# The first 24 microseconds of a hybrid attention and recurrence block: second token block in halves, weight split on three engines, projection steps between transposes

## The chip, the cores and the metric

The kernel runs on one core of a Trainium2 chip. The metric is the device time of one execution in microseconds (us). The core's engines are TensorE (PE: matrix products and transposes, with the weight loads shown apart as PEld), VectorE (DVE), ScalarE (ACT), GpSimd (POOL) and SyncE (SP, which here only issues DMAs). Each engine runs its own instructions in order; semaphores make it wait for the others.

## The reference

One layer on 1024 tokens of width 1024, all in float32:

```python
xn = rmsnorm(x, norm1_g[layer])
u = xn @ w_in[layer].astype(f32)
q_sb, k_sb, v_sb, f_raw, i_hg, q_hg, g_hg, gate_sb, gate_hg = jnp.split(u, list(c), axis=-1)
o_sb = stick_breaking_attention(...)        # 8 heads of 64, needs q_sb, k_sb, v_sb
o_hg = hgrn2_chunkwise(...)                 # 4 heads of 128
merged = g_a * (o_sb @ w_o_sb) + g_b * (o_hg @ w_o_hg)
h = x + merged @ w_out
h = h + square(relu(rmsnorm(h, norm2_g) @ w_ff1)) @ w_ff2
return rmsnorm(h, final_g)
```

The change touches only the beginning: the root-mean-square norm of the tokens, its transposition, and the first projections (query and key of head 0, and v of all heads).

## The kernel before, in words

**Split operands.** Products are made in fp32r, a rounded form of float32. To keep the accuracy each operand is split into a high part (a cast to fp32r, made by ACT, `hi_copy`, L155) and a low part (the source minus the high part, made by DVE, `lo_sub`, L158), and each product is three matmuls, high x high, high x low and low x high (`three`, L566). So ACT and DVE have to feed PE with two tiles per operand.

**Token blocks.** The tokens lie in 8 blocks `x0` to `x7` of 128 rows (tokens) by 1024 columns. A block is normed by its own rows: the sum of squares of each row, then the power -0.5 of it on POOL (`inv_root`, L272), giving one factor per row (`n_y` in the profile), then a scaling of the block in place. For blocks 0 to 3 ACT squares the left half of a block and DVE the right half (`half_means`, L621); an addition on DVE joins the two sums. PE transposes the scaled blocks in 128x128 pieces into PSUM (`xnt`, `norm_transpose`, L322); out of PSUM ACT makes the high part times the norm's gain (`xnh`, L348) and DVE the low part (`xnl`, L351). There are 8 column blocks, called kt; one PSUM bank takes a column block of all token blocks that are transposed together (two in the front). The kernel's pool of PSUM banks has 8.

**The first job.** `first_job` (L724) makes the projections that come first, in steps that the main program orders with `st.advance(n, ...)`: (1) query and key of head 0 for blocks 0 and 1, four steps of two kt each (`pjqk` in the profile, 24 products of 128x256); (2) a part of v for blocks 0 and 1, kt 0 to 3, in four quarters: both products with the high weights for kt 0 and 1, the same for kt 2 and 3, then the product with the low weights for kt 0 and 1, and for kt 2 and 3 (`pjv`, 128x512); (3) query and key for blocks 2 and 3, four steps; (4) the rest, beginning with the epilogue of query and key (two casts on ACT, two subtractions on DVE, and two DMAs from POOL's queue that copy rows 0 to 63 to rows 64 to 127, L682).

The weights of query and key, `wqk0r`, come in four DMAs, two for each half (kt 0 to 3, kt 4 to 7), and are split in two halves (`FirstUnit.split`, L717): high parts `wqk0whi` on ACT, low parts `wqk0wlo` on DVE. The weights of v, `wvr`, come in four pieces of two kt each and are split into `wvh` and `wvl`; the low part of the second piece is put off (`owed_wlo`, L487) until `lo_now` (L141) is called.

**What sets the order.** The DMAs are issued by SP in the written order (`load`, L135). While `turns["on"]` holds, as it does in the whole front, the instructions of ACT and of DVE that pass through `in_turn` (L147) form one fixed chain per engine in the written order. PE's instructions are in two lanes, "main" (transposes, attention) and "fill" (projections); within a lane the order is fixed, and a fill block may not run ahead of the main block two before it (`open_block`, L110). Between the lanes, and on POOL, a planner, which runs when the program is built, settles the order by the written place as a priority and by its own model of when operands are ready. The main program of the front, L2316 to L2344, is this:

```python
first_norms((0, 1))
norm_transpose(xn, 0, 0, 2, lambda: keep_warm(1))
st.advance(4, 1)
u_v.split(2)
norm1((2, 3), half_means((2, 3)))
lo_now()
st.advance(3, 1)
norm_transpose(xn, 0, 2, 2)
u_v.split()
st.advance(5, 1)
norm1(range(4, NT))
```

`keep_warm` issues products of the identity that nobody uses. Behind the front come the attention, the recurrence, the output projection and the MLP, which the diff leaves alone.

Of the kernel before, what the change touches and what calls it, by code (L numbers as in the profile page):

```python
# [9 lines left out]
F32 = mybir.dt.float32  # L10
# [29 lines left out]
def kernel(  # L40
# [160 lines left out]
    def load_x(tb):  # L201
        xt.append(slot(f"x{tb}"))
        load(xt[tb], X[tb * P : (tb + 1) * P, :])
# [118 lines left out]
    def norm_transpose(acts, half, b0, n, between=None):  # L322
# [17 lines left out]
        for kt in range(KT):  # L340
# [18 lines left out]
            )  # L359

# [210 lines left out]
    def proj_half(ps, hl, mov, nk, half, wcol=lambda k: k * P, ts=slice(0, 512)):  # L571
        wh, wl = hl
        for kt in range(nk):
            c = wcol(kt)
            xh, xl = (t[:, ts] for t in mov(kt, half))
            three(ps, wh[:, c : c + P], wl[:, c : c + P], xh, xl, kt == 0, kt == nk - 1)
            if kt % 2 == 1:
                yield
# [42 lines left out]
    def half_means(tbs):  # L621
        (l, lc), (r, rc) = halves()
        means = {}
        for tb in tbs:
            t, scr = xt[tb], slot(f"n1scr{tb}")
            ssq = small.tile([P, 1], F32, tag="ssq1", name=f"n1_{tb}_ss", bufs=4)
            in_turn(
                "act",
                nc.scalar.activation(
                    scr[:, lc], t[:, lc], AF.Square, scale=D ** -0.5, accum_out=ssq  # L630
                ),
            )
            ms = mean_square(scr[:, rc], t[:, rc], EPS, f"n1_{tb}")
            in_turn("dve", add(ms, ms, ssq))
            means[tb] = inv_root(ms, f"n1_{tb}")
        return means

    def first_norms(tbs):
        (l, lc), (r, rc) = halves()
        means = half_means(tbs)  # L640
        for tb in tbs:
            first = tb == tbs[0]
            if first:
                t = xt[tb][:, rc]
                in_turn("act", nc.scalar.activation(t, t, AF.Copy, scale=means[tb]))
            t = xt[tb][:, lc] if first else xt[tb]
            in_turn(
                "dve",
                nc.vector.tensor_scalar(
                    out=t, in0=t, scalar1=means[tb], scalar2=None, op0=ALU.mult  # L650
                ),
            )
            if first:
                turn_vectors(0, 1)
        for part in range(2):
            u_qk0.split(part)

    def norm1(tbs, means=None):
        for tb in tbs:
            t = xt[tb]  # L660
            r = means[tb] if means else token_rstd(t, f"n1_{tb}", slot(f"n1scr{tb}"))
# [39 lines left out]
    class FirstUnit(Unit):  # L701
# [15 lines left out]
        def split(self, part=None):  # L717
            if part is None:
                return
            cs = slice(part * 512, (part + 1) * 512)  # L720
            (h, l), r = self.hl[0], self.raw[0]
            hi_lo(h[:, cs], l[:, cs], r[:, cs])

    def first_job():  # L724
# [17 lines left out]

        def v_steps(tb, kts):
# [7 lines left out]
        def qk_steps(ps, half, b0, n):  # L751
            ts = slice(b0 * P, (b0 + n) * P)
            return proj_half(ps[:, ts], u_qk.hl[0], xn.mov, KT, half, ts=ts)

        def body():
            ps = bank(f"{name}_0")
            yield from qk_steps(ps, 0, 0, 2)
            for hi in (True, False):
                for k0 in (0, 2):
                    for tb in range(2):  # L760
                        for kt in (k0, k0 + 1):
                            v_part(tb, kt, hi, not hi)
                    yield
            yield from qk_steps(ps, 0, 2, 2)
            ep(ps, 0)
            st.prefetch()
# [1746 lines left out]
```

## Time and profile before

| what | us |
|---|---|
| median of 3 runs | 1421.06 (1420.96 to 1421.10) |
| the profiled execution | 1421.05 |
| its span in the trace | 1419.3 |
| PE busy | 1409.0 |
| DVE busy | 1087.3 |
| ACT busy | 684.4 |
| POOL busy | 147.9 |
| block 0 landed, first square | 4.40 |
| first projection product (query and key, blocks 0 and 1) | 10.02 |
| first v product | 13.11 |
| transposes of blocks 2 and 3 begin | 17.68 |
| all work of blocks 0 to 3 up to the low v products done, next v products begin | 23.83 |

How to read the lines below. A timeline row gives the start in us from the span's start, the duration in us, the engine, the line of the kernel, the operation, the tiles written and read with their shapes, and, behind "x", how many instructions of that kind were put together (for these the duration runs from the first start to the last end). In brackets stands how long the engine was idle before and who released it. A matmul's duration includes its way through the array; a sequence of them starts one every 0.12 us (256 columns) or 0.23 us (512 columns). A row of the chain is the time, the duration and what the end of the program hung on then. A row of the table by stages has the stretch, its length, the busy time and number of instructions on PE, PEld, DVE, ACT and POOL, the granted clock of PE, the share of the DMA engines and the GB/s. A row of groups has the busy time, the mean duration in ns, and the idle time before.

### The profile page before, as it was taken

Reading aid. Unit: us, or ns where it says so; the run is one execution under the profiler, and the core shown is the slowest. Engines: PE = TensorE matmul, PEld = TensorE weight load, DVE = VectorE, ACT = ScalarE, POOL = GpSimd, SP = SyncE. Lnnn points to the kernel's source line nnn. Section 1 sums busy time; section 2 is a strip of 40 time slices with the busy share of each in tenths; the row PEclk is TensorE's granted clock in tenths of the full one; section 3 lists DMA queues with packets and bytes.
Section 4 is the critical chain, followed back from the end, with each engine's and each line's share of the span. In section 5 each row is a group of like instructions: output and inputs, shape, how many; then the busy total and the mean of one; then the engine's idle time right before and its main releaser. Section 6 shows DMA issues by size and latency. Waiting matters only on the chain.

```text
span 1419.3 us, 18799 instructions
## 1 busy us (share of the span) xinstructions
PE 1409.0 (99%) x6848; PEld 1183.7 (83%) x6848; DVE 1087.3 (77%) x1494; ACT 684.4 (48%) x1181; POOL 147.9 (10%) x341
## 2 busy tenths in 40 slices
PE   9999999999999999999999999999999999999997
PEld 8888888888888888888888888888888888888886
DVE  7579988988567888887788897676666657768765
ACT  6356676664243554433344764445444443433343
POOL 3012223210011031000000300000000000000042
PEclk9999999999999999999999999999999999999999
DMA  7024445535135685364585514444446974776825
GB/s 243 26 67 127 106 99 98 107 77 155 60 74 174 221 223 182 123 213 156 163 297 193 185 58 166 163 163 145 140 141 242 355 259 154 275 278 239 275 98 179
DMA packets 163173, 237.72 MB, mean 167 GB/s; under 512 B 26332, under 2 KB 93448, under 8 KB 163080
## 3 DMA queue, kind: packets, MB, share of 16 engines
q1 hardware_dynamic: 146056, 190.37, 40.0%
q0 software_dynamic: 11584, 34.61, 10.0%
q10 hardware_dynamic: 5440, 11.54, 2.3%
q8 instruction: 54, 0.88, 0.2%
q14 instruction: 39, 0.32, 0.1%
HBM read 168.32 MB, written 66.06 MB: 165 GB/s over the span
## 4 chain that ended last, share of the span: by engine, by line
PE 98%; DVE 1%; ACT 1%; POOL 0%; DMA 0%; issue 0%; SPq 0%; DVEq 0%; ACTq 0%
PE pm L128 21%; PE pX L128 9%; PE pW L128 6%; PE pY L128 6%; PE pjqk L128 6%; PE pga L128 4%; PE gX L128 4%; PE gY L128 4%; PE pjf L128 3%; PE pjq L128 3%; PE pys L128 3%; PE pji L128 3%; PE pyh L128 3%; PE pjv L128 3%; PE po L128 3%; PE z L128 2%
## 5 line engine op out<-in xcount | busy, mean ns | idle before, releaser
L156 ACT CAST whid<-w 128x1024 fp32r<-128x1024 f32 x30 | 31.6, 1053 | 154.5 <-PE pm L128 89.8
L826 DVE TENSOR_TENSOR_SCAN rm<-rm,bits 128x511 f32<-128x511 f32 (+7 forms) x72 | 87.3, 1219 | 17.2 <-ACT rm L804 17.1
L128 PE MATMUL pm<-wlod,sh 128*128 128x512 f32 x240 | 93.5, 390 | 0.0
L128 PE MATMUL pm<-whid,sl 128*128 128x512 f32 x240 | 93.4, 389 | 0.0
L128 PE MATMUL pm<-whid,sh 128*128 128x512 f32 x240 | 93.4, 389 | 0.0
L128 PE MATMUL pm<-tl,sh 128*128 128x512 f32 (+1 forms) x210 | 81.3, 387 | 0.0
L128 PE MATMUL pm<-th,sl 128*128 128x512 f32 (+1 forms) x210 | 81.3, 387 | 0.0
L128 PE MATMUL pm<-th,sh 128*128 128x512 f32 (+1 forms) x210 | 81.3, 387 | 0.0
L161 DVE TENSOR_TENSOR wlod<-w,whid 128x1024 fp32r<-128x1024 f32 x30 | 36.7, 1222 | 55.2 <-ACT whid L156 55.1
L161 DVE TENSOR_TENSOR sl<-sa,sh 128x1024 fp32r<-128x1024 f32 x56 | 68.2, 1218 | 0.0
L156 ACT CAST wTh<-pw 128x512 fp32r<-128x512 f32 (+2 forms) x96 | 43.8, 485 | 41.9 <-PE pw L131 41.0
L2141 POOL TENSOR_SCALAR fss<-fss 128x1 f32<-128x1 f32 x8 | 4.5, 561 | 562.0 <-ACT fsc L2136 561.5
L156 ACT CAST sh<-sa 128x1024 fp32r<-128x1024 f32 x56 | 57.2, 1046 | 7.0 <-DMA sa<-ad 7.0
L128 PEld LDWEIGHTS pm<-wlod,sh 128*128 128x128 f32 x240 | 45.0, 187 | 9.9 <-DVE wlod L161 0.4
L128 PEld LDWEIGHTS pm<-whid,sh 128*128 128x128 f32 x240 | 45.1, 188 | 9.4
L161 DVE TENSOR_TENSOR wTl<-pw,wTh 128x512 fp32r<-128x512 f32 (+2 forms) x96 | 49.9, 546 | 3.9 <-ACT wTh L156 3.7
L128 PEld LDWEIGHTS pm<-whid,sl 128*128 128x128 f32 x240 | 45.1, 188 | 9.3
L169 DVE TENSOR_TENSOR bt<-bt,rm 128x511 f32<-128x511 f32 (+7 forms) x72 | 48.9, 684 | 3.5
L804 ACT ACTIVATE rm<-z 128x511 f32<-128x511 f32 (+4 forms) x96 | 48.0, 500 | 5.5 <-PE z L128 2.9
L128 PE MATMUL pX<-sql,t1h 128*128 128x512 f32 x128 | 49.9, 390 | 0.0
L128 PE MATMUL pX<-sqh,t1l 128*128 128x512 f32 x128 | 49.9, 390 | 0.0
L128 PE MATMUL pX<-sqh,t1h 128*128 128x512 f32 x128 | 49.8, 389 | 0.0
(930 smaller groups left out, 4435.9 us busy)
## 6 DMA issues: line engine op xcount, KB each, us to landing
w<-in_w_ff_dram SPq DMA_DIRECT2D x72, 512.0 KB, 4.8
sa<-ad SPq DMA_DIRECT2D x52, 512.0 KB, 6.4
ad<-a SPq DMA_DIRECT2D x32, 256.0 KB, 4.6
ad<-s SPq DMA_DIRECT2D x16, 512.0 KB, 3.3
tw<-in_w_out_dram POOLq DMA_DIRECT2D x24, 256.0 KB, 4.6
pr<-pd SPq DMA_DIRECT2D x10, 512.0 KB, 6.5
x<-in_x_dram SPq DMA_DIRECT2D x8, 512.0 KB, 7.8
xnl<-xnh POOLq DMA_DIRECT2D x8, 512.0 KB, 6.4
```

The lines of the kernel that those rows point to most:

```text
L128: return pe(nc.tensor.matmul(*a, **k))
L156: hi_last[0] = after(in_turn("act", nc.scalar.copy(dst, src)), hi_behind[0])
L161: nc.vector.tensor_tensor(out=dst, in0=src, in1=hi.bitcast(F32), op=ALU.subtract),
L169: return nc.vector.tensor_tensor(out=out, in0=a, in1=b, op=ALU.mult)
L804: nc.scalar.activation(rm[:, s0 + c0 - 1 : s0 + m - 1], z[:, c0:m], AF.Sigmoid, scale=-0.125)
L826: sc = nc.vector.tensor_tensor_scan(out=rr, data0=rr, data1=bits[:, 1024 - nk + a : 1024 - nk + b][:, ::-1], initial=rm[:, b : b + 1] if i ...
L2141: nc.gpsimd.tensor_scalar(out=ssq, in0=ssq, scalar1=1.0 / D, scalar2=EPS, op0=ALU.mult, op1=ALU.add)
```

## The change

Six edits, all in the front:

1. Block 1 is loaded by two DMAs, columns 0 to 511 and 512 to 1023, instead of one.
2. Of blocks 0 to 3 ACT squares the end of the row and DVE the beginning. For block 1 DVE squares columns 0 to 511, then 512 to 767 (the second sum starts from the first), and ACT 768 to 1023.
3. Block 1 is scaled by ACT (right half) and DVE (left half), as block 0 already was. The high part of the first half of `wqk0` comes on ACT between the scalings of blocks 0 and 1, that of the second half behind them; the low part of the first half is made by DVE, that of the second half by POOL.
4. For blocks 2 and 3 one power on POOL takes both sums (`second_norms`); ACT scales the left half of block 2, DVE the other three halves.
5. In the query and key products of the first four blocks the product with the low part of the activations comes last of the three.
6. The steps of query and key for blocks 2 and 3 are set among their transposes, behind kt 4, 6 and 7; the put-off low part of v's second piece is made behind the transposes' `xnl`; the last of the four quarters of v follows the query and key steps and their epilogue, which comes ahead of the norms of blocks 4 to 7.

```diff
     def load_x(tb):
         xt.append(slot(f"x{tb}"))
-        load(xt[tb], X[tb * P : (tb + 1) * P, :])
+        for i in range(2) if tb == 1 else (None,):
+            cs = slice(None) if i is None else slice(i * 512, (i + 1) * 512)
+            load(xt[tb][:, cs], X[tb * P : (tb + 1) * P, cs])
...
-    def norm_transpose(acts, half, b0, n, between=None):
+    def norm_transpose(acts, half, b0, n, between=None, then=None):
...
+            if then:
+                then(kt)
...
-    def three(ps, wh, wl, xh, xl, first, last, goes_on=False):
+    def three(ps, wh, wl, xh, xl, first, last, goes_on=False, xl_last=False):
+        rest = ((wh, xl), (wl, xh))
         matmul(ps, wh, xh, start=first, stop=False, skip_group_check=goes_on)
-        matmul(ps, wh, xl, start=False, stop=False, skip_group_check=goes_on)
-        matmul(ps, wl, xh, start=False, stop=last, skip_group_check=goes_on)
+        for i, (w, t) in enumerate(rest[::-1] if xl_last else rest):
+            matmul(ps, w, t, start=False, stop=last and i == 1, skip_group_check=goes_on)
...
-    def half_means(tbs):
+    def half_means(tbs, together=False):
...
+            cuts = (0, 512, 768) if tb == 1 else (0, 512)
+            last = slice(cuts[-1], D)
             in_turn(
                 "act",
                 nc.scalar.activation(
-                    scr[:, lc], t[:, lc], AF.Square, scale=D ** -0.5, accum_out=ssq
+                    scr[:, last], t[:, last], AF.Square, scale=D ** -0.5, accum_out=ssq
                 ),
             )
-            ms = mean_square(scr[:, rc], t[:, rc], EPS, f"n1_{tb}")
+            ms = EPS
+            for a, b in zip(cuts, cuts[1:]):
+                ms = mean_square(scr[:, a:b], t[:, a:b], ms, f"n1_{tb}_{a}")
...
+        if together:
+            nc.gpsimd.tensor_tensor(out=roots, in0=sums, in1=expo[:, 0:2], op=ALU.pow)
         return means
 
     def first_norms(tbs):
...
         for tb in tbs:
...
+            scale_act(xt[tb][:, rc], means[tb])
+            scale_dve(xt[tb][:, lc], means[tb])
+            if tb == tbs[0]:
                 turn_vectors(0, 1)
-        for part in range(2):
-            u_qk0.split(part)
...
+                u_qk0.split_hi(0)
+        u_qk0.split_lo(0, nc.vector)
+        u_qk0.split_hi(1)
+        u_qk0.split_lo(1, nc.gpsimd)
...
+    def second_norms(tbs):
+        (l, lc), (r, rc) = halves()
+        means = half_means(tbs, together=True)
+        a, b = tbs
+        scale_act(xt[a][:, lc], means[a])
+        scale_dve(xt[b][:, lc], means[b])
+        scale_dve(xt[b][:, rc], means[b])
+        scale_dve(xt[a][:, rc], means[a])
...
         def body():
             ps = bank(f"{name}_0")
             yield from qk_steps(ps, 0, 0, 2)
-            for hi in (True, False):
-                for k0 in (0, 2):
-                    for tb in range(2):
-                        for kt in (k0, k0 + 1):
-                            v_part(tb, kt, hi, not hi)
-                    yield
+            for hi, k0 in ((True, 0), (True, 2), (False, 0)):
+                v_quarter(hi, k0)
+                yield
             yield from qk_steps(ps, 0, 2, 2)
             ep(ps, 0)
+            v_quarter(False, 2)
+            yield
             st.prefetch()
...
     u_v.split(2)
-    norm1((2, 3), half_means((2, 3)))
+    second_norms((2, 3))
+    st.advance(3, 1)
+    norm_transpose(xn, 0, 2, 2, then=lambda kt: st.advance(1, 1) if kt in (4, 6, 7) else None)
     lo_now()
-    st.advance(3, 1)
-    norm_transpose(xn, 0, 2, 2)
     u_v.split()
-    st.advance(5, 1)
+    st.advance(2, 1)
     norm1(range(4, NT))
```

More of the change, by code (lines that the diff above doesn't have):

```diff
@@ L741, in v_part, with v_quarter @@
                 matmul(ps, sh, wl, start=False, stop=kt == KT - 1)
+        def v_quarter(hi, k0):
+            for tb in range(2):
+                for kt in (k0, k0 + 1):
+                    v_part(tb, kt, hi, not hi)
         def v_steps(tb, kts):
```

63 lines of the change are left out of this document (38 added, 25 removed).

## The prediction

> **What bounds the kernel now.** I read the page first, then where TensorE (PE) is not busy, stage by stage, then the chain of the first 24 us, then its timeline.
>
> ```profile
> span 1419.3 us, 18799 instructions
> ...
> PE 98%; DVE 1%; ACT 1%; POOL 0%; DMA 0%; issue 0%; SPq 0%; DVEq 0%; ACTq 0%
> ```
>
> PE is the bound: 98% of the chain is PE. The edit can therefore win only time in which PE has nothing useful to do in the front. The table of stages (PE is the second figure of each row) shows how much that is.
>
> ```profile
> 0.00:10.02 10.02, 7.50 (x41) 7.02 (x41) 4.86 (x14) 5.75 (x12) 3.50 (x13) 1.00 0.88 260
> 17.68:20.97 3.29, 3.08 (x21) 2.48 (x20) 3.29 (x8) 2.87 (x8) 0.00 (x0) 1.00 1.04 386
> 23.83:60.00 36.17, 36.13 (x176) 29.84 (x175) 23.57 (x54) 19.30 (x38) 7.20 (x15) 1.00 0.22 55
> 60.00:1400.00 1340.00, 1339.65 (x6489) 1124.61 (x6488) 1038.53 (x1388) 643.02 (x1099) 130.36 (x302) 1.00 0.53 169
> ```
>
> From 23.83 to 1400 PE lacks 0.4 us of being busy throughout, so what the front wins or loses stays until the end, and nothing is to be had behind it. Before 10.02 its busy time is warming matmuls and transposes. The chain of the front:
>
> ```profile
> 3.59 4.52 DMA wqk0r<-in_w_in_dram
> ...
> 8.19 0.62 ACT wqk0whi L156
> 8.81 3.03 ACT xnh L348 x8
> 11.84 0.95 ACT wvh L156
> ...
> 17.54 1.13 DVE wvl L161
> 18.67 0.43 DVE xnl L351
> ...
> 21.14 2.86 PE pjqk L128 x24
> ```
>
> Two places can move: **stage one**, up to the first V product at 13.11, which hangs on the landing of the first weights (8.11) and ScalarE (ACT) behind it; and **stage two**, 17.68 to 23.83: 16 transposes, four low V products, 24 projection products.
>
> **Stage one, part by part.**
>
> ```profile
> 5.81 0.63 ACT L629 ACTIVATE n1scr<-x 128x512 f32<-128x512 f32 x1 [0.69 <-DMA x<-in_x_dram]
> 6.62 0.16 DVE L1284 TENSOR_TENSOR n_ms<-n_ms,n_ss 128x1 f32<-128x1 f32 x1
> 6.44 0.71 ACT L645 ACTIVATE x<-x,n_y 128x512 f32<-128x512 f32 x1
> 6.85 0.73 POOL L274 TENSOR_TENSOR n_y<-n_ms,expo 128x1 f32<-128x1 f32 x1 [0.77 <-DVE n_ms L1284]
> 7.10 0.62 ACT L156 CAST wqk0whi<-wqk0r 128x512 fp32r<-128x512 f32 x1
> 7.62 0.75 DVE L649 TENSOR_SCALAR x<-x,n_y 128x1024 f32<-128x1024 f32 x1 [0.33 <-POOL n_y L274]
> 8.29 1.29 DVE L161 TENSOR_TENSOR wqk0wlo<-wqk0r,wqk0whi 128x512 fp32r<-128x512 f32 x2
> 9.49 3.22 DVE L351 SCALAR_TENSOR_TENSOR xnl<-xnt,prm,xnh 128x256 fp32r<-128x256 f32 x8
> 10.02 0.38 PE L128 MATMUL pjqk<-xnh,wqk0whi 128*128 128x256 f32 x1 [0.27 <-DVE xnl L351]
> 13.11 0.40 PE L128 MATMUL pjv<-wvh,xnh 128*128 128x512 f32 x1
> ```
>
> *Block 1 in halves.* Its second half cannot land before the whole did (5.81). VectorE (DVE) squares the first half before that and 256 columns after it, ACT 256: the sum at 6.62 comes some 0.05 to 0.2 us sooner. This buys nothing by itself: block 1's scaling, now shared, ends near 8.4 on ACT, and the next thing late is ACT's own queue. That queue becomes: scale block 0, first high cast (0.62, begun at 7.10 at the latest), scale block 1 (0.66 from 6.44 to the next instruction at 7.10), second high cast (0.62), then the casts xnh. So 7.10 + 0.62 + 0.66 + 0.62 puts the first xnh at 9.00; if the first weights landed sooner than 7.10, the landing at 8.11 still holds it at 8.81. I take 8.90, 0.09 late: the new scaling does not fit into the 0.47 us (7.72 to 8.19) for which ACT idles now.
>
> *One DMA issue more on SP* stands ahead of the norm vector and the four weight loads:
>
> ```profile
> 2.06 2.04 SPq L136 DMA_DIRECT2D wqk0r<-in_w_in_dram  x4
> ```
>
> One of these issues takes 0.5, and the last landed 4.5 us after its issue, so the transfer queue, not the issue, sets the landing. The bytes are the same. I take 0; the other end is 0.45 later. The loads queued behind shift by one issue as well; block 2 is first wanted behind ACT's wvh casts, after 12.8.
>
> *Low parts on two engines.* DVE now makes both before the xnl (8.29 to 9.58). It keeps one, hidden between its half of block 1's scaling (done by 8.0: 7.5 for the power, half of 0.75 behind it) and 8.65; the other goes to POOL. The xnl then start right behind the first xnh, 0.51 after its start as in stage two (18.10 to 18.61, below): 8.90 + 0.51 = 9.41 instead of 9.49, and at 3.22 for eight end at 12.63, where they ended at 12.71. They still pace PE, one per 0.39 us (3.22 with the last one's 0.48) against three products of 0.12 (2.86 for 24). With the low activations last, one product instead of two follows the last xnl: PE is through at 12.8. The V products need the first wvh, by the chain done 3.98 behind the start of the first xnh (11.84 + 0.95 against 8.81), so at 12.88: **V starts at 12.90 instead of 13.11, 0.21 won** (0.3 with the first xnh at 8.81, a loss of 0.15 with the weights 0.45 late).
>
> *POOL's subtraction* is in no row: 512 columns, two inputs.
>
> ```profile
> L2151 POOL TENSOR_TENSOR y<-hb,gf 128x256 f32<-128x256 f32 x2 | 1.9, 960 | 1.0 <-DVE hb L1284 1.0
> 5.53 0.56 POOL L274 TENSOR_TENSOR n_y<-n_ms,expo 128x1 f32<-128x1 f32 x1 [2.74 <-DVE n_ms L1284]
> L274 POOL TENSOR_TENSOR n_y<-n_ms,expo 128x1 f32<-128x1 f32 x4 | 3.0, 769 | 10.9 <-DVE n_ms L1284 10.9
> ```
>
> Twice the 256 columns gives 1.92 us at most by that row; the powers, 0.56 alone and 0.77 on average, say that POOL is stretched when DVE works, so the bounds are DVE's 0.65 for the same work (1.29 for two) and 1.92 x 1.6 = 3.1 (3.08 for four powers, less 0.56 and 0.73, leaves 0.9 for each of the others, 1.6 times 0.56). I take 1.9, near to its own row: from 8.95 to 10.85. PE wants it at the second product of the fifth column block, 11.3 (the fourth xnl ends at 9.41 + 0.48 + 3 x 0.39 = 11.07, then two products): 0.45 us of cover.
> The Trainium skill, GPSIMD Engine Reference, section "Engine selection", advises against this very move: elementwise work on two inputs belongs on VectorE, GpSimd being about half as fast; section "Elementwise" gives 2.6 cycles per element at 1.2 GHz, from which I estimate 1.1 us, and by that the sum stays as it is. Its section "Key points" says that the engines contend when a DVE instruction has two SBUF inputs or a two-port mode; xnl reads one operand from PSUM, so by that rule POOL would not be stretched here, and no run shown tests it.
>
> **Stage two, part by part.**
>
> ```profile
> 15.63 0.16 DVE L1284 TENSOR_TENSOR n_ms<-n_ms,n_ss 128x1 f32<-128x1 f32 x1
> 15.96 1.58 DVE L664 TENSOR_SCALAR x<-x,n_y 128x1024 f32<-128x1024 f32 x2 [0.17 <-POOL n_y L274]
> 16.77 1.07 PE L128 MATMUL pjv<-wvl,xnh 128*128 128x512 f32 x4
> 17.45 1.22 DVE L161 TENSOR_TENSOR wvl<-wvr,wvh 128x1024 fp32r<-128x1024 f32 x1
> 17.68 1.25 PE L131 MATMUL xnt<-ident,x 128*128 128x128 f32 x10
> 18.10 3.03 ACT L348 ACTIVATE xnh<-xnt,prm 128x256 fp32r<-128x256 f32 x8 [3.15 <-PE xnt L131]
> 18.61 3.23 DVE L351 SCALAR_TENSOR_TENSOR xnl<-xnt,prm,xnh 128x256 fp32r<-128x256 f32 x8
> 22.10 2.36 DVE L161 TENSOR_TENSOR wvl<-wvr,wvh 128x1024 fp32r<-128x1024 f32 x2 [0.26 <-ACT wvh L156]
> 23.83 0.40 PE L128 MATMUL pjv<-wvh,xnh 128*128 128x512 f32 x1
> ```
>
> Minimum work of PE: 16 transposes at some 0.11 (ten in 1.25, the drain of the last included) 1.76, four V products 0.91 (16.77 to 17.68), 24 projection products 2.86: 5.53 against 6.15 spent from 17.68 to 23.83. So 0.62 lie open; the edit sets projection steps into them.
>
> *One power, shared scaling.* The joint power waits for block 3's sum (15.79); with DVE quiet it takes 0.56 and ends near 16.45. ACT's half of block 2 is ready near 17.2 (0.71), DVE's three halves at 0.4 each by 17.7, in the order in which the transposes want them. PE comes there at 17.68 - 0.21 = 17.47: the scaling stays hidden, with 0.2 to spare.
>
> *The moved low part.* The wvl at 17.45 goes behind the eight xnl on DVE, whose order is a fixed chain. This does not start the xnl sooner, because the first needs the first xnh, which began at 18.10 and leaves nothing over when it ends. From 17.47: 0.42 to the first xnh (17.68 to 18.10), 0.51 to the first xnl, 3.22 for eight: 21.62. The last transpose pair stands behind two projection steps (12 products, 1.43 of PE), which pushes the last xnl some 0.35 back, to 21.97, if the planner keeps the written order. I take 21.83. Then wvl, 1.18 (half of 2.36): 23.01; then PE's four products, 0.05 + 0.91: **23.97 where it was 23.83, 0.14 lost** (bounds -0.1 to +0.3). All 24 projection products are through by 22.2, so PE waits some 0.8 us for wvl; the products behind are chained to that quarter and cannot pass it. Thus the 0.62 that the interleaving fills opens again behind it. The last two wvl come at 24.2 and 25.4; PE wants them at 24.4 and 25.8 (two V products of 0.23, then six more): covered.
>
> *The epilogue's move.* Its two ACT casts, two DVE subtractions and two DMAs on POOL's queue now precede the norms of blocks 4 to 7.
>
> ```profile
> 25.18 0.75 DVE L664 TENSOR_SCALAR x<-x,n_y 128x1024 f32<-128x1024 f32 x1 [0.72 <-POOL n_y L269]
> 29.26 0.95 POOL L693 DMA_DIRECT2D QH<-QH  x1
> 29.34 0.75 DVE L664 TENSOR_SCALAR x<-x,n_y 128x1024 f32<-128x1024 f32 x1 [0.72 <-ACT wqk1h L156]
> 34.74 3.65 PE L131 MATMUL xnt<-ident,x 128*128 128x128 f32 x32
> ```
>
> If POOL keeps the written order, the powers wait for DVE's QL (25.4 + 1.3 for two subtractions) and its DMA: 27.65. Block 4 is then scaled near 28.5, and block 7 three rounds of 1.39 (25.18 to 29.34) later, at 32.7 instead of 29.34, done by 33.4, still ahead of its transposes at 34.74: cost 0. DVE's work for V behind them moves by about 1 us; if PSUM banks then come late for the transposes, some 0.2.
>
> **Sum.** -0.21 at the end of stage one, +0.35 from there to the end of stage two: +0.14. The profiled execution took 1421.05, 1.75 more than its span; the median is 1421.06. So 1421.2.
>
> **Rivals.**
> - *Slower: POOL sets the pace* (0.20). If its subtraction takes longer than 2.3 us, PE waits at the fifth column block; at 3.1 it ends at 12.05, eleven products of 0.12 follow, and V starts at 13.37, 0.26 late instead of 0.21 early. The whole of stage two moves by these 0.47: 1421.7. For it: the powers stretched beside DVE. Against: the nearest row leaves 0.45 of cover.
> - *Slower: the extra issue counts, or what lies behind the front shifts* (0.20). Weights 0.45 late give 1421.5; late banks or another order by the planner 1421.4 to 1422.4. For it: PE's order in the trace is not the written one (low V products stand among the last transposes). Against: 0.4 us of idle PE in 1376.
> - *Faster: wvl does not bind* (0.15). If the last xnl and wvl come so that PE never waits, 0.21 + 0.62 are won: 1420.2. Against: DVE's fixed chain.
> - *No effect of any size* (0.05): both stages wait as before, 1421.06.
>
> The forecast keeps 0.40, its own range 1420.9 to 1421.4. The range 1420.1 to 1422.3 takes in the rivals with the bounds. Every priced case lies within 0.2%, 2.8 us, about what a measurement of this kernel can tell from no change; only a new order of the planner far behind could leave it: same 0.91, slower 0.06, faster 0.03.
>
> **What would show it.** Right: first V product near 12.9; first xnh 8.8 to 9.0; a POOL subtraction near 1.9 that nobody waits for; PE waiting about 0.8 for DVE's wvl near 22; V's later products from 23.9. Wrong: PE waiting for POOL near 11.3; no wait for wvl; a wait of PE after 34.

## The result and the profile after

The kernel after takes **1423.76 us** (median of 22 runs, 1423.26 to 1424.22) against 1421.07 before (22 runs, 1420.51 to 1421.79): ratio 1.0019, 95% interval 1.0013 to 1.0025. It is 2.7 us slower, and 1.5 above the upper end of the forecast's range. The page, and three stretches of the table by stages (columns as in the prediction):

```profile
span 1422.0 us, 18805 instructions
...
PE 96%; DVE 1%; DMA 1%; ACT 1%; issue 0%; POOL 0%; SPq 0%; ACTq 0%; DVEq 0%; POOLq 0%
```

```profile
0.00:10.25 10.25, 7.62 (x42) 6.92 (x42) 4.54 (x15) 5.83 (x12) 4.36 (x14) 1.00 0.87 255
17.91:24.73 6.82, 6.07 (x45) 5.54 (x44) 5.98 (x12) 5.94 (x12) 0.00 (x0) 1.00 1.00 286
...
35.62:40.50 4.88, 4.36 (x35) 3.86 (x34) 3.40 (x8) 3.61 (x9) 0.00 (x0) 1.00 0.36 107
```

The span grew by the same 2.7. PE lacks 0.75 us of being busy in stage two (17.91 to 24.73; before, 0.21 in the 6.15 us from 17.68), and 0.5 us in the transposes of blocks 4 to 7 (35.62 to 40.50); before, it lacked nothing in the stretch that holds these transposes.

PE executes 6848 products and transposes in both kernels, in the same order behind the front. So I took the start of the same PE instruction in two traces and subtracted. The table gives how much later than before each kernel reaches six landmarks, named by their times in the kernel before (the experiments are told below):

| kernel | 13.11 | 17.68 | 23.83 | 38.69 | 62 | 495 |
|---|---|---|---|---|---|---|
| after | +0.11 | +0.22 | +0.90 | +1.87 | +1.89 | +2.47 |
| e1_whole | +0.24 | +0.35 | +1.03 | +1.97 | +1.98 | +2.48 |
| e2_norms_first | +0.61 | +0.71 | +1.40 | +1.40 | +1.37 | +2.01 |
| e3_vlow_pool | +0.42 | +2.60 | +2.32 | +3.70 | +3.69 | +4.23 |
| e4_stage_one | +0.29 | +0.40 | +0.55 | +0.56 | +0.55 | +0.47 |
| e5_copies_later | +0.20 | +0.29 | +0.98 | +0.96 | +0.92 | +1.48 |
| e6_halves_only | +1.48 | +1.46 | +1.46 | +1.46 | +1.46 | +1.40 |
| e7_pad | +0.25 | +0.24 | +0.25 | +0.26 | +0.23 | +0.68 |
| e8_best | -0.20 | -0.11 | -0.41 | -0.10 | -0.11 | -0.25 |
| e9_vlow_behind | +0.33 | +0.40 | +0.07 | +1.44 | +1.39 | +1.80 |
| e10_old_places | +0.53 | +0.62 | +1.30 | +2.24 | +2.21 | +2.39 |
| e11_even_whole | -0.27 | -0.20 | +0.07 | +0.07 | +0.09 | +0.17 |
| e12_row_halves | +3.20 | +3.19 | +3.19 | +3.19 | +3.15 | +3.13 |
| e13_extra_issue | -0.08 | -0.10 | -0.10 | -0.10 | -0.10 | -0.10 |
| e14_pad64 | -0.01 | -0.03 | -0.02 | -0.01 | -0.01 | +0.26 |
| e15_pad256 | +0.18 | +0.15 | +0.15 | +0.15 | +0.14 | +0.12 |

Read the rows by their steps, not by their levels: up to 13.11 a single execution also carries the luck of its first load (e7_pad changes nothing there and has +0.25). That luck can be taken out: block 0 landed, by its first square on ACT, between 4.26 and 4.58 in all of these traces but that of e12_row_halves. Counted from that landing, the first V product of e7_pad, e13, e14 and e15, which leave the engines' work in front of it as it was, comes within 0.08 of before's; that of after comes 0.25 late, that of e11 and e8 0.29 and 0.30 early.

After loses in four places: **0.22** up to the end of stage one (17.68), **0.68** in stage two, **0.97** between 23.83 and 38.69, and **0.58** little by little between 62 and 495. That is 2.45 of 2.7; nearly all of the rest lies in the last 30 us, where the traces of the kernels differ by -0.4 to +0.3 with no order to it. The 0.22 is the least certain of the four: block 0 landed early in this trace (4.26, before 4.40), and four kernels with the same edits in front (e2, e5, e9 and e10) have 0.29 to 0.71 at 17.68.

**Stage one** in the timeline of after:

```profile
5.50 0.69 DVE L283 CUSTOM_DVE_ANT_0 n1scr<-x 128x512 f32<-128x512 f32 x1 [0.28 <-DMA x<-in_x_dram]
6.32 0.42 ACT L641 ACTIVATE n1scr<-x 128x256 f32<-128x256 f32 x1 [1.33 <-DMA x<-in_x_dram]
7.26 0.73 POOL L276 TENSOR_TENSOR n_y<-n_ms,expo 128x1 f32<-128x1 f32 x1 [1.32 <-DVE n_ms L1331]
7.55 0.62 ACT L156 CAST wqk0whi<-wqk0r 128x512 fp32r<-128x512 f32 x1
8.08 0.72 ACT L672 ACTIVATE x<-x,n_y 128x512 f32<-128x512 f32 x1
8.70 0.60 ACT L156 CAST wqk0whi<-wqk0r 128x512 fp32r<-128x512 f32 x1
9.21 1.56 ACT L350 ACTIVATE xnh<-xnt,prm 128x256 fp32r<-128x256 f32 x4
9.38 1.27 POOL L761 TENSOR_TENSOR wqk0wlo<-wqk0r,wqk0whi 128x512 fp32r<-128x512 f32 x1 [1.39 <-ACT wqk0whi L156]
13.22 0.50 PE L128 MATMUL pjv<-wvh,xnh 128*128 128x512 f32 x1
```

Block 1's second half lands at 6.32, half a microsecond behind the landing of the whole block before (5.81); the first high cast begins at 7.55 instead of 7.10; all of ACT's queue is late by it.

**Stage two and the epilogue** in the same timeline:

```profile
17.91 1.25 PE L131 MATMUL xnt<-ident,x 128*128 128x128 f32 x10
21.53 0.48 ACT L350 ACTIVATE xnh<-xnt,prm 128x256 fp32r<-128x256 f32 x1 [0.31 <-PE xnt L131]
22.04 0.48 DVE L353 SCALAR_TENSOR_TENSOR xnl<-xnt,prm,xnh 128x256 fp32r<-128x256 f32 x1 [0.28 <-ACT xnh L350]
22.44 3.49 DVE L161 TENSOR_TENSOR wvl<-wvr,wvh 128x1024 fp32r<-128x1024 f32 x3
23.71 1.18 PE L128 MATMUL pjv<-wvl,xnh 128*128 128x512 f32 x4 [0.75 <-DVE wvl L161]
24.73 0.39 PE L128 MATMUL pjv<-wvh,xnh 128*128 128x512 f32 x1
25.40 0.76 POOL L724 DMA_DIRECT2D QH<-QH  x1 [8.44 <-ACT QH L156]
26.67 0.68 DVE L161 TENSOR_TENSOR QL<-pjqk,QH 64x512 fp32r<-64x512 f32 x1
27.66 0.52 POOL L724 DMA_DIRECT2D QL<-QL  x1 [1.50 <-DVE QL L161]
29.14 0.75 DVE L695 TENSOR_SCALAR x<-x,n_y 128x1024 f32<-128x1024 f32 x1 [1.79 <-POOL n_y L271]
33.55 0.75 DVE L695 TENSOR_SCALAR x<-x,n_y 128x1024 f32<-128x1024 f32 x1 [0.71 <-POOL n_y L271]
34.22 1.22 DVE L161 TENSOR_TENSOR wqk1l<-wqk1r,wqk1h 128x1024 fp32r<-128x1024 f32 x1
35.35 0.42 DVE L161 TENSOR_TENSOR V<-pjv,V 128x256 fp32r<-128x256 f32 x1
39.16 0.63 PE L131 MATMUL xnt<-ident,x 128*128 128x128 f32 x4 [0.33 <-DVE V L161]
39.98 0.50 PE L128 MATMUL pjv<-wvh,xnh 128*128 128x512 f32 x1 [0.20 <-DVE xnl L353]
```

Two waits in brackets stand where before had none. At 23.71 PE has waited 0.75 for the low part that was moved behind the `xnl`. At 39.16 it waits for DVE's copy of V out of PSUM, and the line goes back to POOL: QL's DMA stands in POOL's queue ahead of the powers of blocks 4 to 7, is issued only when DVE has made QL (26.67 + 0.68; the issue begins at 27.66), and holds the powers; the last scaling comes at 33.55 instead of 29.34, and the V copies behind it on DVE at 35.35. The two waits of PE there, 0.33 and 0.20, are less than the 0.97 of the table, because a product's way through the array counts as busy: from start to start PE has 0.60 before 39.16 and 0.46 before 39.98, where the same two intervals were 0.11 and 0.03 in the kernel before. The V copies began here in the kernel before:

```profile
32.58 0.41 DVE L161 TENSOR_TENSOR V<-pjv,V 128x256 fp32r<-128x256 f32 x1
```

**The body.** PE's timeline at the same two products of before, and of after:

```profile
61.92 0.40 PE L128 MATMUL pjv<-wvh,xnh 128*128 128x512 f32 x1
...
495.18 0.39 PE L128 MATMUL pho<-k,q 128*128 128x128 f32 x2
```

```profile
63.81 0.40 PE L128 MATMUL pjv<-wvh,xnh 128*128 128x512 f32 x1
...
497.64 0.39 PE L128 MATMUL pho<-k,q 128*128 128x128 f32 x2
```

The stretch takes 433.26 before and 433.83 after, with the same instructions in the same order and no new wait. What differs is where the tiles lie: the sums and the roots of `second_norms` are two new small tiles, in a pool that the program opens ahead of the large ones, so that these lie further on in each partition: by 128 bytes, if each of the two takes 64 (counted from the kernel; no trace shows addresses).

### The profile page after: what moved, and what is told of

It reads as the page before. It is cut to its first block, busy times and chain, and to the rows that moved or that the text cites. A ratio compares the mean times of both kernels' runs of the same rounds, so it can differ in the third digit from the quotient of the medians.

```text
span 1422.0 us, 18805 instructions
## 1 busy us (share of the span) xinstructions
PE 1410.3 (99%) x6848; PEld 1184.2 (83%) x6848; DVE 1086.6 (76%) x1496; ACT 685.6 (48%) x1183; POOL 141.7 (10%) x341
## 4 chain that ended last, share of the span: by engine, by line
PE 96%; DVE 1%; DMA 1%; ACT 1%; issue 0%; POOL 0%; SPq 0%; ACTq 0%; DVEq 0%; POOLq 0%
PE pm L128 19%; PE pX L128 9%; PE pW L128 6%; PE pY L128 6%; PE pjqk L128 6%; PE pga L128 4%; PE gX L128 4%; PE gY L128 4%; PE pjv L128 3%; PE pjf L128 3%; PE pjq L128 3%; PE pys L128 3%; PE pji L128 3%; PE pyh L128 3%; PE po L128 3%; PE z L128 2%
```

## The experiments

Theory: four separate losses (the split load; the wait for `wvl`; QL's DMA ahead of the powers; the places of the tiles). Rivals: the late front itself causes what comes behind it; the order of the weights' parts or the steps among the transposes is at fault. Every kernel but e3 (5 runs) had 11 runs; medians are given beside before's on the same chip; the ratios' intervals reach about 0.0009 to either side, so a median alone settles little below 1.3 us, and each reading rests on its step in the table too.

**1. e1_whole**: after, with block 1 by one DMA.

```diff
-        for i in range(2) if tb == 1 else (None,):
-            cs = slice(None) if i is None else slice(i * 512, (i + 1) * 512)
-            load(xt[tb][:, cs], X[tb * P : (tb + 1) * P, cs])
+        load(xt[tb], X[tb * P : (tb + 1) * P, :])
```

> The changed kernel with block 1 loaded by one DMA again (the sums in three parts stay). Theory (the split load is late): in the trace of the changed kernel the second half of block 1 lands at 6.3, 0.55 us later than the whole block before (5.8), so ACT's first xnh starts at 9.21 instead of 8.81. With one DMA the second sum is ready 0.45 us sooner, the first xnh starts at 8.9 to 9.0, the first V product near 12.95, and the time falls by 0.3 us from 1423.76 to about 1423.45. Rival (ACT's own queue, with the scaling of block 1 put into it, sets the start, whatever lands): first xnh still at 9.2, time within 0.1 of 1423.76.

1423.54 (before 1421.10; ratio 1.0018, 1.0009 to 1.0027). The time came near the expectation, the mechanism did not: the weights are on time again (first high cast at 7.19), but DVE now squares 512 and then 256 columns behind the landing, so the sum's last addition begins at 7.19 instead of 6.62, and the first xnh comes at 9.33 instead of the expected 8.9 to 9.0. Cutting the square in three pays only if the halves land apart.

**2. e2_norms_first**: after, with the norms of blocks 4 to 7 written ahead of the epilogue.

```diff
-    st.advance(2, 1)
+    st.advance(1, 1)
     norm1(range(4, NT))
-    st.advance(8, 1)
+    st.advance(9, 1)
```

> The changed kernel with the norms of blocks 4 to 7 ahead of the epilogue of query and key on ACT, DVE and POOL, as before; PE's order is that of the changed kernel. Theory (held norms): in the changed kernel POOL's powers for blocks 4 to 7 stand behind the epilogue's two DMAs, block 7 is scaled at 33.6 instead of 29.3, V's low parts and with them PSUM banks come late, and PE loses 0.99 us between its transposes at 35.6 and its V products at 40. That loss goes: about 1422.8. Rival (DVE is late by itself, because wvl stands behind xnl): PE loses the same near 38, time within 0.3 of 1423.76. If the 0.6 us that PE loses in small steps between 80 and 490 comes from which buffers the epilogue's tiles get, that goes too: about 1422.2.

1422.98 (ratio 1.0014, 1.0005 to 1.0022), and the step from 23.83 to 38.69 is 0.00 instead of 0.97. The loss from 62 to 495 stays (0.64), so it does not come from the epilogue's buffers.

**3. e3_vlow_pool**: after, with `wvl` of the second piece on POOL.

```diff
-                    owed_wlo.append(lambda h=h, l=l, r=r: lo_sub(l, r, h))
+                    owed_wlo.append(
+                        lambda h=h, l=l, r=r: nc.gpsimd.tensor_tensor(
+                            out=l, in0=r, in1=h.bitcast(F32), op=ALU.subtract
+                        )
+                        if self.name == "wv"
+                        else lo_sub(l, r, h)
+                    )
```

> The changed kernel with the moved low part of v's second piece made by POOL instead of DVE. Theory (PE waits for that wvl): the wait of 0.75 us at 23.7, with 0.2 of issue around it, goes: PE's four low V products follow the projection products at 22.8, next V products at 23.8 instead of 24.7. The last two wvl and the epilogue on DVE come 1.2 us sooner, so part of the later loss at 35 to 40 goes too: 1422.0 to 1422.8. Rival (PE waits there for another thing, or POOL's 2.5 us take the place): time within 0.2 of 1423.76.

1426.28 (5 runs; before 1421.10; ratio 1.0037, 1.0023 to 1.0051). Both expectations missed, and inconclusive for the wait: the planner set POOL's subtraction ahead of the joint power, beside DVE's square of block 2. The timeline of e3_vlow_pool:

```profile
14.51 2.49 POOL L492 TENSOR_TENSOR wvl<-wvr,wvh 128x1024 fp32r<-128x1024 f32 x1 [3.54 <-ACT wvh L156]
14.65 2.89 DVE L283 CUSTOM_DVE_ANT_0 n1scr<-x 128x512 f32<-128x512 f32 x1
```

The square takes 2.89 instead of 0.69: longer by 2.2, nearly the length of POOL's operation. The Trainium skill, SBUF — State Buffer, section "A bandwidth-pool intuition that's wrong (but worth ruling out)", says that a GpSimd operation and a DVE operation that uses two ports do not run at the same time: one of them fully blocks. The row agrees, if the square, which names the block as both of its inputs, is such an operation; here it was DVE that waited.

**4. e4_stage_one**: before, with the first stage's edits (1, 2, 3 and 5) alone; as a diff against after:

```diff
...
-    second_norms((2, 3))
+    means = half_means((2, 3))
+    for tb in (2, 3):
+        scale_dve(xt[tb], means[tb])
...
```

(and the steps behind it, and the four quarters of v, in before's order).

> The kernel before with the edits of stage one alone (block 1 in halves and squared in three parts, its scaling on two engines, the first weights' low parts on DVE and POOL, low activations last); stage two as before. Theory (split load late, ACT's queue later): first V product 0.2 to 0.3 us late, everything behind shifted by that: 1421.3. Rival (stage one by itself is a gain, as was forecast): 1420.9 or less. A third reading (a new layout of buffers slows the attention by 0.6): 1421.9.

1421.77 (before 1421.10; ratio 1.0006, 0.9997 to 1.0015): later than the theory's 1421.3, and by the time alone nearest to the third reading. The table decides against that reading: stage one and stage two lose (0.40 and 0.15), and with before's places there is no drift (0.55 at 62, 0.47 at 495), which the rival of a late front would need too.

**5. e5_copies_later**: after, where only the epilogue's two DMAs on POOL wait until behind the powers.

```diff
...
-                nc.gpsimd.dma_start(Q[64:128, cs].bitcast(F32), Q[0:64, cs].bitcast(F32))
+            def copies(behind=None):
...
+                    dma = nc.gpsimd.dma_start(Q[64:128, cs].bitcast(F32), Q[0:64, cs].bitcast(F32))
+                    after(dma, behind)
...
     norm1(range(4, NT))
+    owed_copies.pop()(last_power[0])
```

> The changed kernel with only the epilogue's two DMAs on POOL's queue put behind the powers of blocks 4 to 7; the epilogue's casts on ACT and subtractions on DVE stay ahead. Theory A (POOL's queue holds the norms: their first instruction could start at 26.2 and starts at 28.3): most of the loss between 35.6 and 40 goes, 0.6 to 1.0: 1422.8 to 1423.2. Theory B (the casts and subtractions in front do it): within 0.25 of 1423.76.

1422.87 (before 1421.09; ratio 1.0013, 1.0004 to 1.0022). The epilogue's casts and subtractions stay where the change puts them, and the step from 23.83 to 38.69 is gone (-0.02). Its timeline:

```profile
27.34 0.73 DVE L695 TENSOR_SCALAR x<-x,n_y 128x1024 f32<-128x1024 f32 x1
...
33.54 0.42 DVE L161 TENSOR_TENSOR V<-pjv,V 128x256 fp32r<-128x256 f32 x1
```

The first scaling and the V copies come 1.8 us sooner than in after. So POOL's queue was the cause, worth 0.89.

**6. e6_halves_only**: before, with the split load alone (edit 1).

> The kernel before with only the load of block 1 in two DMAs. Theory (split load late by 0.6 to 0.9 behind block 0's landing, and the first weights 0.35 behind that): block 1's sum, power and scaling, all in line with DVE's low parts and xnl, shift by 0.5 to 0.8, PE's first product from 10.02 to about 10.6: 1421.6 to 1421.9 against 1421.1. Rival (the two halves take as long as the whole, the traces differ by chance): within 0.15 of 1421.1.

1421.95 (before 1421.09; ratio 1.0007, 0.9998 to 1.0016): 0.86 lost by the medians. The interval touches 1, but all 11 runs lie above 32 of the 33 of before. Its second half of block 1 is there at 6.50 (before, the whole block at 5.81):

```profile
6.50 0.69 DVE L283 CUSTOM_DVE_ANT_0 n1scr<-x 128x512 f32<-128x512 f32 x1 [1.10 <-DMA x<-in_x_dram]
```

What the DMAs moved from 3.5 to 4.5 us, in before, after and e6_halves_only, by the DMA view of each:

```profile
DMA packets 111, 0.39 MB, mean 393 GB/s; under 512 B 15, under 2 KB 15, under 8 KB 111
```

```profile
DMA packets 105, 0.20 MB, mean 205 GB/s; under 512 B 8, under 2 KB 8, under 8 KB 105
```

```profile
DMA packets 116, 0.26 MB, mean 264 GB/s; under 512 B 12, under 2 KB 12, under 8 KB 116
```

About as many packets, but most of 2 KB instead of 4 KB: in this microsecond the rate falls to half or two thirds, and block 1's end and the weights behind it are late. The small packets alone do not explain it. In the next half microsecond after still moves 2 KB packets, and its rate is that of before (the rows of the table by stages, before and after):

```profile
4.50:5.00 0.50, 0.50 (x5) 0.50 (x4) 0.50 (x1) 0.50 (x2) 0.00 (x0) 1.00 0.90 354
```

```profile
4.50:5.00 0.50, 0.50 (x5) 0.50 (x4) 0.46 (x2) 0.48 (x2) 0.00 (x0) 1.00 1.02 347
```

So the loss lies where the halves begin to move.

**7. e7_pad**: before, with 128 bytes per partition of unused tiles ahead of all others; **14. e14_pad64** and **15. e15_pad256**: the same with 64 and 256 bytes.

```diff
     xt = []
+    for i in range(2):
+        small.tile([P, 2], F32, tag=f"pad{i}", name=f"pad{i}")
```

(`range(1)` for 64 bytes, `range(4)` for 256).

> The kernel before, each engine's instructions and their order the same, with 128 bytes of unused small tiles in each partition, so that nearly all SBUF tiles lie 128 bytes away, as in the changed kernel, whose two new small tiles move them. Theory (the 0.5 to 0.6 us that PE loses in steps of 0.01 from 80 to 490 in the runs with stage two's edits, and not in the run with stage one's alone, come from where the tiles lie): 0.4 to 0.6 over 1421.1, in the same stretch. Rival (they come from the edits' timing): within 0.15 of 1421.1.

> Before with an unused tile of 64 bytes per partition ahead of all others, so that the tiles move by 64 bytes; instructions and order are before's. Theory (any move by less than 256 bytes costs PE's 512-column products some time): the lead from 62 to 495 us grows by 0.3 to 0.6, time 1421.3 to 1421.6. Rival (only 128 bytes do it): no drift, time 1421.0 to 1421.1.

> Before with 256 bytes per partition of unused tiles ahead of all others. Theory (the place within some 256 bytes counts): no drift from 62 to 495 us, time 1421.0 to 1421.1. Rival (a move of any size counts): drift 0.3 to 0.6, time 1421.3 to 1421.6.

1421.50 with 128 bytes (ratio 1.0002, 0.9993 to 1.0011), 1421.47 with 64 (1.0003, 0.9994 to 1.0012), 1421.18 with 256 (1.0000, 0.9991 to 1.0009), before 1421.09 to 1421.11. PE's timeline with 128 and with 256 bytes:

```profile
62.15 0.40 PE L128 MATMUL pjv<-wvh,xnh 128*128 128x512 f32 x1
...
495.85 0.39 PE L128 MATMUL pho<-k,q 128*128 128x128 f32 x2
```

```profile
62.06 0.40 PE L128 MATMUL pjv<-wvh,xnh 128*128 128x512 f32 x1
...
495.29 0.39 PE L128 MATMUL pho<-k,q 128*128 128x128 f32 x2
```

433.70 with 128 bytes and 433.23 with 256, against 433.26 in the kernel before (64 bytes: 0.27 more). Of the 2383 intervals between starts of products in this stretch, 146 are over 4 ns longer than before with 128 bytes, 141 in after, 15 with 256. So where the tiles lie costs time, and a move by 256 bytes costs none. The medians follow the traces (0.41, 0.36 and 0.07 over before with 128, 64 and 256 bytes), though their intervals alone would not show it.

**8. e8_best**: after, but block 1 whole and squared in two halves, scaled by DVE; one low part of `wqk0` on POOL and edit 5, as in after; single powers; `wvl` of the second piece on POOL behind block 3's scaling; steps among the transposes as in after; norms of blocks 4 to 7 ahead of the epilogue; no new tile.

```diff
+    def pool_lo(l, r, h):
+        seen = nc.gpsimd.tensor_copy(lmx[:, 0:1], xt[3][:, D - 1 : D])
+        return after(
+            nc.gpsimd.tensor_tensor(out=l, in0=r, in1=h.bitcast(F32), op=ALU.subtract), seen
+        )
...
```

> A version put together from what the runs showed: block 1 in one DMA and squared in halves and scaled by DVE, as before; the second low part of the first weights on POOL and low activations last, as changed; single powers and DVE's scaling for blocks 2 and 3, as before (tiles where they lay); projection steps among the transposes and the last v quarter behind them, as changed, with the low part of v's second piece on POOL, behind the scaling of block 3; norms of blocks 4 to 7 ahead of the epilogue, as before. Theory (every loss has a cause of its own, and each is left out here): first V product near 12.9, no wait for wvl, next V products near 23.1, nothing later: 1420.3 to 1420.6. Rival (POOL's work on two inputs holds DVE, as in the run with v's low part on POOL, where a square on DVE took 2.9 instead of 0.7): 1421.1 or more.

1420.77 (1420.43 to 1421.20; before 1421.09; ratio 0.9997, 0.9988 to 1.0006): 3.0 below after, and 0.3 below before by the medians, which the interval doesn't tell from no change, though ten of its eleven runs lie below the lowest of before's 33 (1420.89). Its list of PE's waits has none in the front but that for the identity at the start, and the later V products begin at 23.42:

```profile
17.82 2.37 POOL L144 TENSOR_TENSOR wvl<-wvr,wvh 128x1024 fp32r<-128x1024 f32 x1
18.54 2.92 DVE L357 SCALAR_TENSOR_TENSOR xnl<-xnt,prm,xnh 128x256 fp32r<-128x256 f32 x7 [0.93 <-ACT xnh L354]
...
23.42 0.39 PE L128 MATMUL pjv<-wvh,xnh 128*128 128x512 f32 x1
```

Beside POOL's subtraction the `xnl`, which read one operand from PSUM, keep their pace (the first seven take 2.92, and 2.93 in after).

**9. e9_vlow_behind**: after, with e8's subtraction on POOL, behind the scaling of block 2's right half (the last of the four), and nothing else changed.

> After, with v's low part of piece 2 (wvl, 3.49 us on DVE when it was made by line 161) made by POOL instead, behind a tiny POOL copy of block 2's last scaled columns, so that no two-input work of POOL lies beside the norms' squares. Theory (the wait for wvl at 23.71 costs the second stage some 0.7 to 0.95): PE finds wvl ready, the lead to before at 23.83 falls from +0.90 to +0.2, and the time is 1422.8 to 1423.0. Rival (something else in the second stage costs it, xnl of block 3 or the order of the steps): the wait moves to xnl, and the time stays at 1423.6 to 1423.8.

1422.95 (before 1421.05; ratio 1.0012, 1.0003 to 1.0021). The wait at 23.71 is gone, and from 17.68 to 23.83 the kernel gains 0.33 on before, where after loses 0.68. But 0.4 of this 1.0 is given back by 38.69 (+1.37 instead of +0.97): the later V products begin 0.82 sooner than in after (23.91 against 24.73), QL's DMA only 0.41 sooner (27.25 against 27.66), for the subtractions on DVE ahead of it wait for ACT's casts of `wvh`, which do not come sooner.

**10. e10_old_places**: after, with the sums and roots written into columns of a tile that is there already.

```diff
-            sums = small.tile([P, 2], F32, tag="means2", name="n1_sums")
-            roots = small.tile([P, 2], F32, tag="roots2", name="n1_roots")
+            sums, roots = le[:, 0:2], le[:, 2:4]
```

> After, with the two new small tiles (two sums, two roots) written into columns 0 to 3 of a tile that is there already (le), so that no tile of SBUF moves against before; instructions and their order stay. Theory (places of the tiles cost 0.4 to 0.6 in the body's 512-column products): the drift from 62 to 495 us goes from +0.58 to about 0, and the time is 1423.1 to 1423.4. Rival (the drift comes from the late front or by chance): the time stays at 1423.6 to 1423.8.

1423.23 (before 1421.05; ratio 1.0014, 1.0006 to 1.0023); from 62 to 495 it loses 0.18 instead of 0.58. That is most of the drift, not all of it; where the 0.18 comes from stays open.

**11. e11_even_whole**: e4, with block 1 loaded whole as in e1, and squared in two even halves.

```diff
...
-            cuts = (0, 512, 768) if tb == 1 else (0, 512)
+            cuts = (0, 512)
...
```

> Before with the change's first stage alone, but block 1 loaded whole and squared in two even halves as before; block 1's scaling shared by ACT and DVE, wqk0's four parts in the change's order with one low part on POOL. My prediction's working of the first stage without its split: block 1's scaling done 0.4 earlier, first V product at 12.9 instead of 13.1, time 1420.8 to 1420.9. Rival (the split of the square into three and the split load are not what loses; the order of the weights' parts is): the first stage is as late as in the kernel with all edits of the first stage, time 1421.4 to 1421.8.

1421.04 (before 1421.05; ratio 0.9999, 0.9990 to 1.0008). The first stage does what the prediction worked out for it, and its gain doesn't last:

```profile
8.82 1.92 ACT L348 ACTIVATE xnh<-xnt,prm 128x256 fp32r<-128x256 f32 x5
...
12.84 0.48 PE L128 MATMUL pjv<-wvh,xnh 128*128 128x512 f32 x1
17.55 1.22 DVE L161 TENSOR_TENSOR wvl<-wvr,wvh 128x1024 fp32r<-128x1024 f32 x1
18.69 3.22 DVE L351 SCALAR_TENSOR_TENSOR xnl<-xnt,prm,xnh 128x256 fp32r<-128x256 f32 x8
23.91 0.40 PE L128 MATMUL pjv<-wvh,xnh 128*128 128x512 f32 x1
```

In before's stage two, which this kernel has, DVE is the bound: its `wvl` stays at 17.55 (17.45 before) and holds the `xnl`, though PE is there 0.2 sooner. DVE could not come sooner, for its work on blocks 2 and 3 hangs on ACT, whose first xnh is where it was (8.82; before 8.81).

**12. e12_row_halves**: before, with block 1 in two DMAs of 64 rows each.

```diff
-        load(xt[tb], X[tb * P : (tb + 1) * P, :])
+        for i in range(2) if tb == 1 else (None,):
+            rs = slice(0, P) if i is None else slice(i * 64, (i + 1) * 64)
+            load(xt[tb][rs], X[tb * P + rs.start : tb * P + rs.stop, :])
```

> Before with block 1 loaded by two DMAs of 64 rows with all 1024 columns, instead of one of 128 rows; squares as before, so both are needed by each square. Theory (a second issue and its completion cost, whatever the packets' size): block 1 lands 0.4 to 0.6 later, time 1421.4 to 1421.7. Rival (2048-byte packets of the column halves cost it): block 1 lands as before, time 1421.0 to 1421.2.

1424.05 (before 1421.05; ratio 1.0020, 1.0011 to 1.0029): both expectations missed, 3.0 lost. Over the first 9 us the DMA view gives

```profile
DMA packets 2174, 1.52 MB, mean 169 GB/s; under 512 B 1908, under 2 KB 1916, under 8 KB 2174
```

against 243 GB/s before. The Trainium skill, SBUF — State Buffer, section "Door 1: The DMA port swizzle", states that rows 0 to 63 reach only half of the 16 SBUF ports, and rows 64 to 127 the other half; the fall agrees in its direction, though no run here tells ports from other causes. As a test of edit 1 the run decides nothing, since it changed more than the number of transfers: block 0, which it loads as before, lands at 5.66 instead of 4.40.

**13. e13_extra_issue**: before, with one tiny DMA more on SP between block 1 and the norm vector.

```diff
+        if i == 0:
+            load(prow[0][64:72, :], norm1_g[0].rearrange("(a b) -> a b", b=P))
```

> Before with one tiny DMA more on SP (4 KB, the norm vector a second time into rows that nobody reads), issued behind block 1 and ahead of the norm vector and the first weights; all tiles stay where they are. Theory (the issue itself delays what is issued behind it): block 1 lands as before (about 5.8), the first weights' high casts start some 0.4 to 0.5 later (8.6 for the second instead of 8.19), first V product some 0.4 late, time 1421.4 to 1421.5. Rival (the column halves' packets delay the weights, the issue is hidden behind the transfers): casts as before, time 1421.0 to 1421.1.

1421.25 (before 1421.11; ratio 1.0001, 0.9992 to 1.0010):

```profile
2.38 2.05 SPq L136 DMA_DIRECT2D wqk0r<-in_w_in_dram  x4
...
8.06 0.62 ACT L156 CAST wqk0whi<-wqk0r 128x512 fp32r<-128x512 f32 x1 [0.41 <-DMA wqk0r<-in_w_in_dram]
```

The weights are issued 0.32 later than before, yet the second high cast, which waits for them, begins no later (8.06; before 8.19); counted from block 0's landing (4.26; before 4.40) the two agree to 0.01. So the issue ahead of the weights is hidden, as the rival said. What it is about the two halves that slows them is not separated: smaller packets, two transfers in place of one, or the second half's own issue, which begins at 1.64 where that of the whole block began at 1.17.

## Why the prediction was wrong, point by point

The forecast was a change too small to tell, +0.14, and the kernel lost 2.7. That the sign came out right is luck: the sum was a gain of 0.21 and a loss of 0.35, and the gain did not come. The rival of the extra issue and of what lies behind the front named two of the four places, at 1421.5 and at most 1422.4. Of its signs of being wrong one came, a wait of PE after 34 (39.16); of its signs of being right the POOL subtraction that nobody waits for and the wait for `wvl` came. By its own steps:

- **"The bytes are the same. I take 0."** The step that failed in stage one. The issue is hidden, as it said (e13: within 0.14), but two halves are not the same load: from 3.5 to 4.5 us 393 GB/s fell to 205, block 1 ended at 6.32 to 6.50 instead of 5.81, and the step alone cost 0.86 in before's arrangement (e6). In after the first V product comes 0.11 late where 0.21 were to be won. The square in three parts, which was to make the sum sooner, belongs to it: with the block whole it makes the sum later (e1). The "other end" of 0.45 bounded the issue; no bound was set on the rate.
- **"0.21 won" by V at 12.90** was right for the other edits: without the split and the three-part square V starts at 12.84, the first xnh at 8.82 (forecast 8.90; e11). Whether it stays won depends on stage two, which the prediction worked out for the change's order alone: with before's order, where DVE is the bound, 0.27 are given back (e11), with the steps among the transposes and `wvl` on POOL they are not (e8, -0.41 at 23.83).
- **POOL's subtraction, 1.9**: 1.27, with nobody waiting. The estimate of 1.1 from the Trainium skill (GPSIMD Engine Reference, section "Elementwise") was nearer than the one from the nearest row.
- **"+0.35" in stage two**: mechanism right, size 0.68. The wait is 0.75 (forecast 0.8). The last `xnl` ends 4.61 behind the first transpose (22.04 + 0.48 - 17.91), where 4.36 were forecast: the two steps ahead of the last transposes push it by 0.46, beyond the 0.35 thought of. The four products behind the wait take 1.02 instead of 0.91.
- **"cost 0" for the epilogue's move** failed, and is the largest term: 0.97 in the trace, 0.89 by its removal. The row was foreseen (powers behind QL's DMA at 27.65: 27.66), the rounds came as 1.47 instead of 1.39. But the prediction asked only whether block 7 is ready for its transposes; it is, at 34.3. What came late is behind the scalings on DVE, `wqk1l` and the V copies. "If PSUM banks then come late" named it, at 0.2, and the sum left it out; it cost five times that.
- **"Nothing is to be had behind it"** failed for 0.58: a table of busy time cannot show products that each take some ns longer. No edit was priced for where it puts the tiles. e7 and e15 show that a move by 128 bytes costs 0.44 from 62 to 495 and one by 256 bytes nothing; e10 shows that after loses 0.40 less there with the tiles in their old places.

e8, which avoids all four losses in one kernel, is 3.0 faster than after. Open stays why two half loads move at half the rate where they begin, by what mechanism a place within 256 bytes slows products and which, and the 0.2 to 0.3 us in the last 30.

## What to carry to other kernels

When a step is moved, follow each engine's queue behind it to what is last in it, not to the first thing that was due: here a DMA issue on POOL, which waits for DVE, held powers, then scalings, then the copies that free PSUM. A stage's gain counts only as far as the next stage's own bound lets it through. A load cut in halves along its rows' length is another load. And a new tile of some bytes can move all others: compare against a kernel with padding alone before a few tenths are put down to an edit, and count an early landmark from the landing of the first load before a trace is compared with another.

## What the hardware showed that was not expected

- Block 1 as two loads of 512 columns: 205 to 264 GB/s instead of 393 from 3.5 to 4.5 us, and no difference from 4.5 to 5.0 (340 to 347 against 354); as two loads of 64 rows, 3.0 us for the kernel.
- DVE's square of SBUF data beside POOL's subtraction on SBUF: 2.89 instead of 0.69; `xnl` with an operand in PSUM: unchanged.
- Tiles moved by 64, 128 and 256 bytes per partition: +0.27, +0.44 and -0.03 us in 433 us of the same products.
